# A gather by the one-hot as weights, with h split ahead in the projection, in a two-layer trunk with experts

## Chip, cores and metric

The kernel runs on one core of one Trainium2 chip. The metric is device time in microseconds (us) of one execution; three executions of the kernel before are shown, and one profiled execution.

## The reference, cut to what matters

Two layers, each a mixer (layer 0: gated linear attention beside a state-space head group; layer 1: a gated recurrence beside latent attention) and then a channel mixer with 16 experts, of which each of the 256 tokens takes two. x is 256 x 1024.

```python
for layer in (0, 1):
    h = h + g1 * mixer(modulate(h, norm_mix, sh1, sc1))
    xt = modulate(h, norm_ffn, sh2, sc2)              # rms_norm(h) * gain * (1 + scale) + shift
    scores = sigmoid(xt @ router_w)                   # 16 experts; best group of four, then top 2
    combine = normalized weights of the two experts
    for e in range(16):
        hid = silu(xt @ w_gate[e]) * (xt @ w_up[e])
        out += combine[:, e:e+1] * (hid @ w_down[e])
    h = h + g2 * out
```

## The kernel before

All weights come from HBM through one queue, SP's, into a ring of slots of 1 MB (`Stream`, L227). A slot is asked for when the program frees an older one, up to a cap that each stage sets (L20), and if a stretch of the work area is free. Weights of an expert stage are 96 slots: 16 experts with gate, up and down, two slots each. The first three experts have fixed places; the order of the other 13 follows from the routing, so their loads are issued only when 13 numbers have been read into SP's registers (L2030).

The two mixers are scheduled by the compiler; the parts under `manual()` (L303), and so the whole of `moe` (L1904), keep the order in which the program issues them, engine by engine.

`out_proj` (L790) ends a mixer: products in two precisions parts into four banks (token half t, column half c), then `add` (L808) scales them, adds them to h and squares the new h for the norm. `moe` then turns h (L1922), forms the router's logits, the norm's factors `rs`, the routing (L1776) with ranks within each expert, and splits h times `rs` into a high and a low part of reduced-precision type (L1948, L1951). `late` (L545) takes conditioning products (L540) in between.

The experts are worked off in seven passes of 128 token places (L29): two experts with 64 places each, or four with 32, and so on. Pass p has these steps. `one_hot` (L1989) marks on VectorE which token stands in which place, one pass ahead. `gather` (L2009) brings the tokens of the next pass in as columns: for each of eight blocks of 128 features four products (high and low part, two token halves) with h as weights and the one-hot as the moving operand, then scale and shift by feature (L2022, L2024) into `x3`. `hidden` (L2058) makes the gate and up products (L2066), each expert on its own columns of the array, and the gated activation. Between gate and up stands `spread(1)` of the pass before, which puts its results back to the tokens (L2123) and adds them to h (L2124). `turned` (L2083) transposes the one-hot and the hidden rows (L2095, L2096). `down` (L2098) makes the down products of one column half (L2106), scales them (L2109) and splits them in two parts (L2111, L2112). The loop over passes (L2237) has the order: one_hot of the pass after the next, hidden, turned, gather of features 0 to 511, down 0, gather of features 512 to 1023, spread(0), down 1. In the last pass a branch (L2225) is taken or not by a number read at run time, for tokens beyond an expert's places; it has further passes of the same kind (L2131), which don't occur with these inputs.

Of the kernel before, what the change touches and what calls it, by code (L numbers as in the profile page):

```python
# [18 lines left out]
ARENA, ARENAR, ARENAX = 34048, 6144, 5376  # L19
MIX0_CAP, MIX1_CAP, ODD_CAP, PRE_CAP, MOE_CAP = 7, 6, 11, 12, 18  # L20
# [149 lines left out]
class Arena:  # L170
# [6 lines left out]
    def alloc(self, n):  # L177

        fit = [(o + w - n < self.floor, w, -o, i) for i, (o, w) in enumerate(self.free_) if w >= n]
        if not fit:  # L180
            raise RuntimeError('arena full: %d of %s' % (n, self.free_))
        _, w, o, i = min(fit)
        self.free_[i:i + 1] = [(-o, w - n)] if w > n else []
        return Buf(self, w - o - n, n)
# [113 lines left out]
class Trunk:  # L298
# [56 lines left out]
    def sources(self):  # L355
# [13 lines left out]
        def moe(l):  # L369

            def add(place, e, hf):
                c = slice(2048 * hf, 2048 * hf + 2048)

                def late():
                    if self.eids.get(l) is None:
# [87 lines left out]
    def setup(self):  # L463
# [27 lines left out]
        self.cos, self.sin = T(64, 'cos'), T(64, 'sin')  # L491

# [143 lines left out]

    def rstd(self):
        self.nc.vector.scalar_tensor_tensor(self.ss, self.hsq[0], EPS, self.hsq[1], op0=ALU.add, op1=ALU.add)  # L638
        self.pow(self.rs2, self.ss, self.mhalf)
# [126 lines left out]
    def mixer_input(self, x, tmp):  # L766

        nc = self.nc
        self.xhb, self.xlb = self.newx(2048), self.newx(2048)
# [12 lines left out]

    def input_done(self):

        self.x2 = Rot(self.rx, 256, 3), Rot(self.rx, 256, 2)
        self.xhb.free()
        self.xlb.free()
        self.x2[1].b.append(self.newx(256))

    def out_proj(self, nk, mix, hook):  # L790
# [84 lines left out]
    def even_head(self):  # L875
# [24 lines left out]
        self.xhb, self.xlb = self.newx(2048), self.newx(2048)  # L900
# [26 lines left out]
    def even(self):  # L927
# [371 lines left out]
        def hook(k):  # L1299
# [79 lines left out]
    def odd(self):  # L1379
        nc, W, A, new = self.nc, self.W, self.A, self.new  # L1380
        mm, V, S, G = nc.tensor.matmul, nc.vector, nc.scalar, nc.gpsimd
        ident = self.ident
        lwa, lwx = new(1024), new(1024)
        nc.sync.dma_start(lwa.f, A['lwa'])
        nc.sync.dma_start(lwx.f, A['lwx'])
        stat = new(192)
# [82 lines left out]
        ktok, krt, vb = [new(1024) for _ in range(2)], [new(512) for _ in range(2)], new(2048)  # L1469
# [179 lines left out]
        def attn_c(h):  # L1649
# [5 lines left out]
            mix[8 + h] = new(256)  # L1655
# [7 lines left out]
        def lru_gates(f, x):  # L1663
            lb[f] = ab, qb, ub, gb = [new(256) for _ in range(4)]
# [106 lines left out]
        for b in mix.values():  # L1771
            b.free()
# [3 lines left out]
    def route(self, pl, wk, then):  # L1776
# [17 lines left out]
        then()  # L1794
# [44 lines left out]
        key2, cmp, big, res = tmp(NDYN), tmp(n2), tmp(2 * n2), tmp(NDYN)  # L1839
# [64 lines left out]
    def moe(self, l):  # L1904
        nc, W, new = self.nc, self.W, self.new
        mm, V, S, G = nc.tensor.matmul, nc.vector, nc.scalar, nc.gpsimd
        region = self.region('xm%d' % l, 6400)
# [10 lines left out]
        ht, lgs, wk = newf(2048), newf(256), new(800)  # L1918
# [29 lines left out]
        def high(t):  # L1948
            S.activation(hs[0][:, t], self.h[:, t], AF.Identity, scale=self.rs[t])

        def low(t):  # L1951
            V.scalar_tensor_tensor(hs[1][:, t], self.h[:, t], self.rs[t], hh.v(2)[:, t], op0=ALU.mult, op1=ALU.subtract)

# [13 lines left out]
        total(0)  # L1967
        rstd(1)
# [33 lines left out]
        oh = one_hot(0, s3)  # L2002
        low(0)
        low(1)
        xg = newf(1024)
        yh, yl = newx(512), newx(512)
        mcol = self.mcol2

        def gather(one, js=(0, 1), act=False):  # L2009

            ps = [self.ps('gat') for _ in js]
            for q, (t, h) in enumerate((t, h) for h in hs for t in range(2)):
                for j, p in zip(js, ps):
                    for i in range(4):
                        d = slice(128 * (4 * j + i), 128 * (4 * j + i) + 128)
                        mm(p[:, 128 * i:128 * i + 128], h[:, t, d], one[:, t, :], start=q + i == 0, stop=q + i == 6)  # L2016
            for j, p in zip(js, ps):
                for i in range(4):
                    c = 32 * i + j
                    d, x, sc, sh = x3[:, 4 * j + i], p[:, 128 * i:128 * i + 128], mcol[:, c + 8:c + 9], mcol[:, c + 6:c + 7]  # L2020
                    if j and not act:
                        V.tensor_scalar(d, x, sc, sh, op0=ALU.mult, op1=ALU.add)  # L2022
                    else:
                        S.activation(d, x, AF.Identity, scale=sc, bias=sh)  # L2024
        x3 = xg.v(8)
        gather(oh.v(2, True), act=True)
# [11 lines left out]
        wk.free()  # L2038
        hd, htb, uscb = new(512), new(512), new(160)
# [58 lines left out]
        def down(p, c, parts=1):  # L2098

            ws = [weight(base[p] + j, 'wd', c) for j in range(len(PASSES[p]))]  # L2100
            n = 512 // parts
            for i in range(parts):
                py = self.ps('y')
# [4 lines left out]
                s = slice(n * i, n * i + n)  # L2108
                V.scalar_tensor_tensor(xo.f[:, s], py[:, 0:n], self.wc, self.g[:, 512 * c + n * i:512 * c + n * i + n],  # L2109
                                       op0=ALU.mult, op1=ALU.mult)  # L2110
                S.activation(yh.r[:, s], xo.f[:, s], AF.Copy)  # L2111
                V.tensor_tensor(yl.r[:, s], xo.f[:, s], yh.f[:, s], op=ALU.subtract)  # L2112
            W.free(*ws)

# [16 lines left out]
        def unit_hidden(u, ws, ub):  # L2131
# [5 lines left out]
            m, x, su, cu = usc[:, 0:16], usc[:, 16:48], usc[:, 48:50], usc[:, 50:52]  # L2137
# [9 lines left out]
            for t in range(2):  # L2147
                V.tensor_scalar(one[:, t].rearrange('p (j s) -> p j s', j=2),
                                iota[:, 0:64].unsqueeze(1).to_broadcast([128, 2, 64]), su[:, t:t + 1], None, op0=ALU.is_equal)
            for c in range(2):  # L2150
# [6 lines left out]
                if c:  # L2157
                    V.tensor_copy(xu[64:128], p[64:128])
                else:
                    S.activation(xu[0:64], p[0:64], AF.Copy)  # L2160
# [113 lines left out]
        for r in (hh, hl, hd, htb, uscb):  # L2274
# [20 lines left out]
```

## Time and profile before

| what | value |
|---|---|
| three executions | 900.54 us median (899.21 to 900.74) |
| profiled execution | 900.47 us, its span 898.7 us |
| TensorE (PE) busy | 828.0 us, 92% of the span |
| VectorE (DVE) busy | 481.9 us, 54% |
| ScalarE (ACT) busy | 296.8 us, 33% |
| SP's weight queue (q1) | 303.78 MB, 84.0% of 16 engines' span |
| granted TensorE clock | 0.967 of full speed, mean |

Busy times are unions over the span; PE's ends are modelled, so of two products behind each other the starts are the safer measure. PEld is the load of weights into the array, which lies beside products. In a timeline an arrow in brackets gives the idle time of the engine ahead of the instruction and what ended it. In views by stretch PEclk is the granted share of TensorE's full clock, DMA the mean busy share of 16 DMA engines.

### The profile page before, as it was taken

The numbers are of one execution on the slowest core, as the hardware profiler recorded it, in microseconds if no ns is written. First come the engines' busy times: TensorE is split into PE (matmuls) and PEld (weight loads), VectorE is DVE, ScalarE is ACT, GpSimd is POOL, SyncE is SP. The second block draws the span as 40 slices with busy tenths as digits, with TensorE's granted clock in tenths as the row PEclk, the third lists the DMA queues.
The fourth block names the chain that finished last, engine by engine and source line by source line (L and its number), as shares of the span: only waits on it lengthen the run. The fifth ranks groups of instructions, "written<-read, shape, count | busy, mean of one in ns | idle before, by whom it ended". The sixth has DMA issues, their size and how long they took to land. (4 is left out here: it accounts for less than half of the span.)

```text
span 898.7 us, 13799 instructions
## 1 busy us (share of the span) xinstructions
PE 828.0 (92%) x5202; PEld 515.1 (57%) x5202; DVE 481.9 (54%) x1081; ACT 296.8 (33%) x593; POOL 121.6 (14%) x123
## 2 busy tenths in 40 slices
PE   4797999999899999999779899999989999999976
PEld 1686878768543444354248678998845444345422
DVE  3599856986713531233137688998672342233313
ACT  3354335544320111011034468997332111111100
POOL 0044344431000000000004620112100000000000
PEclk9899999999999999999899899999988999999988
DMA  9992786698889999999989388234979999999994
GB/s 373 417 419 108 286 332 261 226 370 332 320 343 421 421 421 419 421 421 420 417 323 389 101 342 353 94 115 135 357 304 420 422 420 420 421 420 421 422 416 178
DMA packets 44431, 306.02 MB, mean 341 GB/s; under 512 B 5057, under 2 KB 5953, under 8 KB 8513
## 3 DMA queue, kind: packets, MB, share of 16 engines
q1 hardware_dynamic: 43344, 303.78, 84.0%
q10 hardware_dynamic: 1008, 1.24, 0.4%
q8 instruction: 44, 0.72, 0.3%
q14 instruction: 35, 0.28, 0.1%
HBM read 303.95 MB, written 1.05 MB: 339 GB/s over the span
## 5 line engine op out<-in xcount | busy, mean ns | idle before, releaser
L2106 PE MATMUL y<-arena 128*64 128x512 f32 (+3 forms) x592 | 109.1, 577 | 4.1 <-DMA arena<-wd 2.7
L2109 DVE SCALAR_TENSOR_TENSOR arena<-y,wc,g 128x512 f32<-128x512 f32 (+1 forms) x30 | 21.5, 716 | 108.8 <-PE y L2106 108.8
L2106 PEld LDWEIGHTS y<-arena 128*32 128x32 f32 (+2 forms) x592 | 34.0, 132 | 61.7 <-issue 48.0
L692 DVE TENSOR_TENSOR x0r<-arena,x0r 128x1024 fp32r<-128x1024 f32 x40 | 56.1, 1404 | 14.8 <-ACT x0r L691 9.5
L2111 ACT ACTIVATE xm<-arena 128x512 fp32r<-128x512 f32 (+1 forms) x30 | 18.1, 602 | 135.6 <-DVE arena L2109 135.6
L2016 PEld LDWEIGHTS gat<-xm 128*128 128x128 f32 x448 | 55.4, 202 | 12.1 <-issue 12.1
L2074 DVE TENSOR_TENSOR arena<-arena,up 128x512 f32<-128x512 f32 x14 | 9.6, 688 | 96.9 <-PE up L2066 96.9
L692 DVE TENSOR_TENSOR x1r<-arena,x1r 128x1024 fp32r<-128x1024 f32 (+3 forms) x52 | 54.4, 1059 | 9.5 <-POOL x1r L689 4.6
L2016 PE MATMUL gat<-xm 128*128 128x128 f32 x448 | 59.3, 289 | 0.0
L2066 PE MATMUL up<-arena,xm0f 128*64 128x512 f32 (+2 forms) x224 | 52.0, 631 | 5.9 <-DVEq L2225 5.9
L2066 PE MATMUL up<-arena,xm1f 128*64 128x512 f32 (+2 forms) x224 | 51.7, 627 | 5.9 <-DVEq L2225 5.9
L2096 ACT ACTIVATE arena<-hidt 128x512 f32<-128x512 f32 x14 | 8.4, 599 | 139.5 <-PE hidt L2095 139.5
L2066 PE MATMUL gate<-arena,xm1f 128*32 128x512 f32 (+2 forms) x240 | 47.2, 604 | 0.0
L2071 DVE SCALAR_TENSOR_TENSOR arena<-arena,gate 128x512 f32<-128x512 f32 x14 | 9.6, 687 | 69.6 <-ACT arena L2070 58.6
L800 PE MATMUL op<-x1r,x 128*128 128x512 f32 x192 | 46.6, 396 | 0.0
L2066 PE MATMUL gate<-arena,xm0f 128*32 128x512 f32 (+2 forms) x240 | 46.1, 594 | 0.1
L691 ACT ACTIVATE x1r<-arena 128x1024 fp32r<-128x1024 f32 (+3 forms) x42 | 37.3, 902 | 22.7 <-PE kv L764 7.5
L2123 PE MATMUL mo<-xm 128*128 128x512 f32 (+1 forms) x120 | 38.5, 421 | 5.6 <-ACT xm L2111 3.9
L540 PE MATMUL adaps<-arena,cpad 128*32 128x512 f32 x320 | 41.6, 640 | 0.0
L619 POOL TENSOR_TENSOR rs<-ss,mhalf 128x1 f32<-128x1 f32 (+1 forms) x6 | 4.5, 750 | 271.0 <-DVE ss L638 246.7
L800 PEld LDWEIGHTS op<-x1r,x 128*128 128x128 f32 x192 | 35.1, 188 | 8.0 <-issue 0.5
L742 PE MATMUL xbc<-x,x0r 128*128 128x256 f32 x264 | 34.1, 286 | 4.8 <-DVE arena L846 2.9
(461 smaller groups left out, 1588.4 us busy)
## 6 DMA issues: line engine op xcount, KB each, us to landing
arena<-wd SPq DMA_DIRECT2D x62, 1024.0 KB, 15.3
arena<-wg SPq DMA_DIRECT2D x56, 1024.0 KB, 12.9
arena<-wu SPq DMA_DIRECT2D x54, 1024.0 KB, 14.1
arena<-ada SPq DMA_DIRECT2D x48, 1024.0 KB, 8.2
arena<-evin SPq DMA_DIRECT2D x16, 1024.0 KB, 11.1
arena<-odout SPq DMA_DIRECT2D x8, 1024.0 KB, 4.8
arena<-odin SPq DMA_DIRECT2D x8, 1024.0 KB, 11.6
arena<-evout SPq DMA_DIRECT2D x6, 1024.0 KB, 5.9
```

Of the source, the lines that this page charges most:

```text
L540: i = self.nc.tensor.matmul(self.aps[32 * k4:32 * k4 + 32, :], self.cpad[:, 32 * (4 * hf + k4) + 31 - n:32 * (4 * hf + k4) + 63 - n], b.f[ ...
L691: nc.scalar.activation(hi, w, AF.Copy)
L692: (nc.gpsimd if d == 'P' else nc.vector).tensor_tensor(lo, w, hi.bitcast(F32), op=ALU.subtract)
L742: self.nc.tensor.matmul(p[:, c0:c0 + 256], a[:, 128 * k:128 * k + 128], b[:, k, :], start=n == 0, stop=n == 23)
L800: nc.tensor.matmul(acc[t][c], x[a][:, ts], w[b][:, 512 * c:512 * c + 512], start=f and k == 0, stop=l and k == nk - 1)
L2016: mm(p[:, 128 * i:128 * i + 128], h[:, t, d], one[:, t, :], start=q + i == 0, stop=q + i == 6)
L2066: mm(ph[o:o + w, :], x(4 * hf + k)[:, o:o + w], ws[j].f[:, 512 * k:512 * k + 512], start=hf + k == 0, stop=hf == 1 and k == 3)
L2071: V.scalar_tensor_tensor(hd.f, hd.f, 1.0, ph, op0=ALU.add, op1=ALU.mult)
L2106: mm(py[o:o + w, 0:n], ht[:, 128 * f + o:128 * f + o + w], ws[j].f[:, 512 * f + n * i:512 * f + n * i + n], start=f == 0, stop=f == 3)
L2109: V.scalar_tensor_tensor(xo.f[:, s], py[:, 0:n], self.wc, self.g[:, 512 * c + n * i:512 * c + n * i + n], op0=ALU.mult, op1=ALU.mult)
L2111: S.activation(yh.r[:, s], xo.f[:, s], AF.Copy)
L2123: mm(po[:, 0:n], cw[:, 128 * t:128 * t + 128], y.r[:, n * i:n * i + n], start=j == 0, stop=j == 1)
```

## The change

Six edits, in the words of the code. (1) `out_proj`'s `add` splits the new h of three of its four quarters into parts by itself, without `rs`; the fourth is split in `moe`. The parts live in a buffer of 4096 columns that the mixers' inputs also use. (2) `scales` makes the norm's factor by place, with the one-hot as weights (two products of one column and a copy); `pick` gathers with the one-hot as weights (four products of 512 columns) and multiplies by that factor; `place` transposes (four) and applies scale and shift. (3) In the loop, `pick` and `place` stand where `gather` stood, `spread(0)` moves behind the second down product, and the end of that product (`y1`) behind `spread(0)`. (4) The conditioning products of the stage's head come all ahead of the routing. (5) The register load is split in one and twelve, each followed by issues. (6) The second mixer's products get one block, some of its buffers other homes, and the ring's cap in the projections is 14.

```diff
-ARENA, ARENAR, ARENAX = 34048, 6144, 5376
-MIX0_CAP, MIX1_CAP, ODD_CAP, PRE_CAP, MOE_CAP = 7, 6, 11, 12, 18
+ARENA, ARENAR, ARENAX = 34048, 6144, 1280
+MIX0_CAP, MIX1_CAP, ODD_CAP, PRE_CAP, MOE_CAP = 7, 6, 11, 14, 18
...
+        self.rsg = T(2, 'rsg')
+        self.kr = Arena(keep.tile([128, 4096], F32R, name='xhl'), 4096, True)
+        self.hp = [Buf(self.kr, 2048 * i, 2048) for i in range(2)]
...
+    def parts(self, t, c):
+
+        s = slice(512 * c, 512 * c + 512)
+        self.split(*[b.v(2, True)[:, t, s] for b in self.hp], self.h[:, t, s])
...
             if t + c < 2:
                 self.square(t, c, acc[t][c])
+                self.parts(t, c)
...
-                W.set_cap(PRE_CAP + 2)
+                W.set_cap(PRE_CAP)
...
+        mixb = self.ar.alloc(4096, True)
+        mixs = [Buf(self.ar, mixb.o + 256 * i, 256) for i in range(16)]
...
-            mix[8 + h] = new(256)
+            mix[8 + h] = mixs[8 + h]
...
-            lb[f] = ab, qb, ub, gb = [new(256) for _ in range(4)]
+            lb[f] = ab, qb, ub, gb = [self.ar.alloc(256, f > 2) for _ in range(3)] + [mixs[f]]
...
-        hh, hl = self.newr(2048), self.newr(2048)
-        hs = (hh.v(2, True), hl.v(2, True))
+        hs = [b.v(2, True) for b in self.hp]
...
         total(0)
+        S.activation(hs[0][:, 1, 512:1024], self.h[:, 1, 512:1024], AF.Copy)
         rstd(1)
...
-        self.late(2)
-
-        def highs():
-            for t in range(2):
-                high(t)
-        sort, combine = self.route(pl[:, 0:32], wk.f, highs)
         self.late(99)
+        sort, combine = self.route(pl[:, 0:32], wk.f)
...
-        oh = one_hot(0, s3)
-        low(0)
-        low(1)
...
+        def scales(dst, one):
+
+            p = self.ps('rsg')
+            for t in range(2):
+                mm(p[:, 0:1], one[:, t], self.rs[t], start=t == 0, stop=t == 1)
+            V.tensor_copy(dst, p[:, 0:1])
+
+        def pick(p, c, xt, act):
+
+            one, pg, r = oh2[p % 2].v(2, True), self.ps('gat'), rsg[:, p % 2:p % 2 + 1]
+            for q, (t, h) in enumerate((t, h) for t in range(2) for h in hs):
+                mm(pg, one[:, t], h[:, t, 512 * c:512 * c + 512], start=q == 0, stop=q == 3)
+            if act:
+                S.activation(xt, pg, AF.Identity, scale=r)
+            else:
+                V.tensor_scalar(xt, pg, r, None, op0=ALU.mult)
+
+        def place(c, xt, act):
+
+            pt = self.ps('xt')
+            for i in range(4):
+                nc.tensor.transpose(pt[:, 128 * i:128 * i + 128], xt[:, 128 * i:128 * i + 128], self.ident)
+            for i in range(4):
+                o = 32 * i + c
+                d, x, sc, sh = x3[:, 4 * c + i], pt[:, 128 * i:128 * i + 128], mcol[:, o + 8:o + 9], mcol[:, o + 6:o + 7]
+                if act:
+                    S.activation(d, x, AF.Identity, scale=sc, bias=sh)
+                else:
+                    V.tensor_scalar(d, x, sc, sh, op0=ALU.mult, op1=ALU.add)
+        one_hot(0, s3)
+        scales(rsg[:, 0:1], oh2[0].v(2))
+        V.tensor_tensor(hs[1][:, 1, 512:1024], self.h[:, 1, 512:1024], self.hp[0].v(2)[:, 1, 512:1024], op=ALU.subtract)
+        pick(0, 0, self.mod, True)
+        pick(0, 1, t1.f, False)
+        place(0, self.mod, True)
+        place(1, t1.f, True)
         sort()
...
-        self.eids[l] = regs(self.cnt[0:1, 0:NDYN], engines=SP, min_val=0, max_val=15)[1]
-        W.fill()
+        self.eids[l] = []
+        for a, b in ((0, 1), (1, NDYN)):
+            self.eids[l] += regs(self.cnt[0:1, a:b], engines=SP, min_val=0, max_val=15)[1]
+            W.fill()
         one_hot(1)
+        scales(rsg[:, 1:2], oh2[1].v(2))
...
-        def down(p, c, parts=1):
+        def down(p, c, parts=1, later=False):
...
+                if not later:
+                    end()
             W.free(*ws)
+            return end
...
             if 0 < p < last:
                 one_hot(p + 1)
+                scales(rsg[:, (p + 1) % 2:(p + 1) % 2 + 1], oh2[(p + 1) % 2].v(2))
...
             if p < last:
-                gather(oh2[(p + 1) % 2].v(2, True), (0,))
+                pick(p + 1, 0, self.mod, True)
             down(p, 0)
             if p < last:
-                gather(oh2[(p + 1) % 2].v(2, True), (1,))
-            spread(0, cw, p == last)
-            down(p, 1, 2 if p == last else 1)
+                place(0, self.mod, True)
+                pick(p + 1, 1, self.mod, False)
+                y1 = down(p, 1, later=True)
+                place(1, self.mod, False)
+                spread(0, cw)
+                y1()
+            else:
+                spread(0, cw, True)
+                down(p, 1, 2)
             before = cw
```

## Rows read from the trace of the kernel before

**Rows 1.** Busy time by stretch, middle of the first expert stage, columns as in the view's head.
```profile
core 0: us, PE busy (x) PEld busy (x) DVE busy (x) ACT busy (x) POOL busy (x), PEclk, DMA share, GB/s
255.00:345.00 90.00, 88.99 (x518) 38.90 (x518) 30.11 (x76) 12.13 (x25) 0.00 (x0) 1.00 1.01 421
```

**Rows 2.** What TensorE waited for, 246 to 460 and 680 to 900: total us, times, longest.
```profile
PE y L2106 <- DMA arena<-wd: 1.8, 2, 1.4
...
PE y L2106 <- DMA arena<-wd: 0.9, 1, 0.9
```

**Rows 3.** Timeline, change from pass 1 to pass 2 of layer 0: start us, length us, engine, line.
```profile
292.67 0.66 PE L2095 MATMUL hidt<-consts,arena 128*128 128x128 f32 x4
...
293.08 1.98 PE L2016 MATMUL gat<-xm 128*128 128x128 f32 x16
...
293.37 0.60 ACT L2096 ACTIVATE arena<-hidt 128x512 f32<-128x512 f32 x1 [9.01 <-PE hidt L2095]
...
300.78 1.36 DVE L2022 TENSOR_SCALAR xm0f<-gat,mcol 128x128 f32<-128x128 f32 x4
...
301.81 3.65 PE L2106 MATMUL y<-arena 128*64 128x512 f32 x16
302.06 1.28 DVE L2124 TENSOR_TENSOR h<-mo,h 128x512 f32<-128x512 f32 x2
305.29 7.04 PE L2066 MATMUL gate<-arena,xm0f 128*64 128x512 f32 x32
```

**Rows 4.** Timeline, the routing of layer 0 on TensorE and of layer 1 on VectorE.
```profile
238.98 0.20 PE L1829 MATMUL rank<-ob,c 128*128 128x16 bf16 x1 [2.83 <-DVE ob L1826]
...
239.27 3.29 PE L540 MATMUL adaps<-arena,cpad 128*32 128x512 f32 x16
...
682.92 0.69 DVE L659 TENSOR_TENSOR modlo<-modrow,modhi 128x512 fp32r<-128x512 f32 x1 [5.37 <-ACT modhi L658]
683.53 0.18 DVE L1868 SCALAR_TENSOR_TENSOR arena<-arena,ob 128x32 f32<-128x32 f32 x1
```

**Rows 5.** Timeline, pass 1 of layer 0, from the end of pass 0 to its up products.
```profile
276.92 0.75 DVE L2109 SCALAR_TENSOR_TENSOR arena<-y,wc,g 128x512 f32<-128x512 f32 x1 [2.20 <-PE y L2106]
...
279.04 0.49 DVE L1997 TENSOR_TENSOR xm<-pslot,consts 128x128 fp32r<-128x128 f32 x2
...
283.64 1.20 PE L2123 MATMUL mo<-xm 128*128 128x512 f32 x4
...
284.77 7.09 PE L2066 MATMUL up<-arena,xm0f 128*64 128x512 f32 x32
```

**Rows 6.** Busy time by stretch: the last pass, and the end of the routing, of layer 0.
```profile
432.50:450.00 17.50, 10.78 (x87) 3.40 (x86) 2.60 (x6) 0.46 (x1) 0.00 (x0) 0.80 1.01 416
...
247.50:250.00 2.50, 2.50 (x14) 0.86 (x12) 1.12 (x4) 1.26 (x4) 0.00 (x0) 1.00 0.04 10
```

**Rows 7.** Timeline of TensorE, last pass of layer 0.
```profile
438.44 1.07 PE L2066 MATMUL up<-arena,xm0f 128*32 128x512 f32 x3 [5.93 <-DVEq L2225]
...
447.91 0.44 PE L2080 MATMUL cw<-consts,xm 128*128 128x128 f32 x2
...
455.37 0.50 PE L2123 MATMUL mo<-xm 128*128 128x512 f32 x1 [1.54 <-ACT xm L2111]
...
456.99 5.35 PE L2106 MATMUL y<-arena 128*32 128x256 f32 x64
```

**Rows 8.** Timeline, first gather and first gate products, layer 0, then layer 1.
```profile
240.01 2.47 DVE L1952 SCALAR_TENSOR_TENSOR xm<-h,rs,xm 128x1024 fp32r<-128x1024 f32 x2
...
246.10 0.49 DVE L1997 TENSOR_TENSOR xm<-pslot,consts 128x128 fp32r<-128x128 f32 x2
...
246.38 7.09 PE L2066 MATMUL gate<-arena,xm0f 128*64 128x512 f32 x32
...
673.20 7.09 PE L2016 MATMUL gat<-xm 128*128 128x128 f32 x32
...
676.46 0.50 DVE L1997 TENSOR_TENSOR xm<-pslot,consts 128x128 fp32r<-128x128 f32 x2
...
680.22 8.15 PE L2066 MATMUL gate<-arena,xm1f 128*64 128x512 f32 x32
```

More of the change, by code (lines that the diff above doesn't have):

```diff
@@ L175, in __init__, with alloc @@
         self.given = [(0, 0, cols)]
-    def alloc(self, n):
-        fit = [(o + w - n < self.floor, w, -o, i) for i, (o, w) in enumerate(self.free_) if w >= n]
+    def alloc(self, n, last=False):
+        fit = [(o + w - n < self.floor, 0 if last else w, -o, i) for i, (o, w) in enumerate(self.free_) if w >= n]
         if not fit:
@@ L182, in alloc @@
         _, w, o, i = min(fit)
+        w = self.free_[i][1]
         self.free_[i:i + 1] = [(-o, w - n)] if w > n else []
@@ L374, in late @@
                 def late():
-                    if self.eids.get(l) is None:
+                    if len(self.eids.get(l, ())) <= place - STATIC:
                         return None
@@ L768, in mixer_input @@
         nc = self.nc
-        self.xhb, self.xlb = self.newx(2048), self.newx(2048)
+        self.xhb, self.xlb = self.kr.alloc(2048), self.kr.alloc(2048)
         self.xh, self.xl = self.xhb.v(8, True), self.xlb.v(8, True)
@@ L787, in input_done @@
         self.xlb.free()
-        self.x2[1].b.append(self.newx(256))
+        self.x2[1].b.append(self.kr.alloc(256))
     def out_proj(self, nk, mix, hook):
@@ L899, in even_head @@
         nc = self.nc
-        self.xhb, self.xlb = self.newx(2048), self.newx(2048)
+        self.xhb, self.xlb = self.kr.alloc(2048), self.kr.alloc(2048)
         self.xh, self.xl = self.xhb.v(8, True), self.xlb.v(8, True)
@@ L1385, in odd @@
         nc.sync.dma_start(lwx.f, A['lwx'])
-        stat = new(192)
+        stat = self.ar.alloc(192, True)
         st = stat.f
@@ L1468, in odd @@
         self.tail()
-        ktok, krt, vb = [new(1024) for _ in range(2)], [new(512) for _ in range(2)], new(2048)
+        ktok, krt, vb = [new(1024) for _ in range(2)], [new(512) for _ in range(2)], self.ar.alloc(2048, True)
         v3 = vb.v(2)
@@ L1770, in odd, with route @@
         self.out_proj(16, lambda k: mix[order[k]].f, hook)
-        for b in mix.values():
-            b.free()
+        mixb.free()
         self.end_phase()
-    def route(self, pl, wk, then):
+    def route(self, pl, wk):
         nc, V, S = self.nc, self.nc.vector, self.nc.scalar
@@ L1793, in route @@
         S.activation(th, th, AF.Tanh, scale=0.5)
-        then()
         V.scalar_tensor_tensor(d3(sel), d3(th), 0.5, self.bias16.unsqueeze(1).to_broadcast([128, 2, 16]),
@@ L1838, in route @@
         n2 = NDYN * NDYN
-        key2, cmp, big, res = tmp(NDYN), tmp(n2), tmp(2 * n2), tmp(NDYN)
+        cmp, big, key2, res = tmp(n2), tmp(2 * n2), kb[:, 0:NDYN], v[:, 0:NDYN]
         sq = lambda a: a.rearrange('p (a b) -> p a b', a=NDYN)
@@ L1906, in moe @@
         mm, V, S, G = nc.tensor.matmul, nc.vector, nc.scalar, nc.gpsimd
-        region = self.region('xm%d' % l, 6400)
+        region = self.region('xm%d' % l, 2304)
         newx, newf = self.newx, self.fx.alloc
         self.dump('h%d' % (1 + 2 * l), flat(self.h))
-        hh, hl = self.newr(2048), self.newr(2048)
-        hs = (hh.v(2, True), hl.v(2, True))
+        hs = [b.v(2, True) for b in self.hp]
         W.more = self.fx
@@ L1917, in moe @@
         oho = newx(256)
-        ht, lgs, wk = newf(2048), newf(256), new(800)
+        ht, lgs, wk, t1 = newf(2048), newf(256), new(768), new(512)
         pl, lg = self.ps('logit'), self.ps('logits')
@@ L1946, in total @@
             mm(pl[:, 16 * t:16 * t + 16], d, self.cst('lsel'), start=True, stop=True)
[L1948 to L1952, printed above, removed]
         def rstd(t):
@@ L2001, in one_hot @@
             return o
-        oh = one_hot(0, s3)
-        low(0)
-        low(1)
-        xg = newf(1024)
+        xg, rsg = newf(1024), self.rsg
         yh, yl = newx(512), newx(512)
[L2007 to L2024, printed above, removed]
@@ L2025, in moe @@
-        x3 = xg.v(8)
-        gather(oh.v(2, True), act=True)
+        mcol, x3 = self.mcol2, xg.v(8)
+        def scales(dst, one):
[11 more added lines that the diff above has]
+                V.tensor_scalar(xt, pg, r, None, op0=ALU.mult)
@@ L2038, in moe @@
         wk.free()
+        t1.free()
         hd, htb, uscb = new(512), new(512), new(160)
@@ L2096, in turned, with end @@
             S.activation(ht, pt, AF.Copy)
-        def down(p, c, parts=1):
+        def down(p, c, parts=1, later=False):
             ws = [weight(base[p] + j, 'wd', c) for j in range(len(PASSES[p]))]
             n = 512 // parts
+            def end():
+                V.scalar_tensor_tensor(xo.f[:, s], py[:, 0:n], self.wc, self.g[:, 512 * c + n * i:512 * c + n * i + n],
+                                       op0=ALU.mult, op1=ALU.mult)
+                S.activation(yh.r[:, s], xo.f[:, s], AF.Copy)
+                V.tensor_tensor(yl.r[:, s], xo.f[:, s], yh.f[:, s], op=ALU.subtract)
             for i in range(parts):
-                py = self.ps('y')
+                py, s = self.ps('y'), slice(n * i, n * i + n)
                 for f in range(4):
@@ L2107, in down @@
                            ws[j].f[:, 512 * f + n * i:512 * f + n * i + n], start=f == 0, stop=f == 3)
[L2108 to L2112, printed above, removed]
+                if not later:
+                    end()
             W.free(*ws)
+            return end
         def spread(c, cw, last=False, parts=1):
@@ L2136, in unit_hidden @@
             ow = hd2.rearrange('p (t s) -> p t s', t=2)
-            m, x, su, cu = usc[:, 0:16], usc[:, 16:48], usc[:, 48:50], usc[:, 50:52]
+            m, x, su, cu, ru = usc[:, 0:16], usc[:, 16:48], usc[:, 48:50], usc[:, 50:52], usc[:, 52:53]
             x3, m3 = x.rearrange('p (t e) -> p t e', t=2), m.unsqueeze(1).to_broadcast([128, 2, 16])
@@ L2149, in unit_hidden @@
                                 iota[:, 0:64].unsqueeze(1).to_broadcast([128, 2, 64]), su[:, t:t + 1], None, op0=ALU.is_equal)
+            scales(ru, ohu)
             for c in range(2):
@@ L2157, in unit_hidden @@
                 if c:
-                    V.tensor_copy(xu[64:128], p[64:128])
+                    V.tensor_scalar(xu[64:128], p[64:128], ru[64:128], None, op0=ALU.mult)
                 else:
-                    S.activation(xu[0:64], p[0:64], AF.Copy)
+                    S.activation(xu[0:64], p[0:64], AF.Identity, scale=ru[0:64])
             for t in range(2):
@@ L2273, in moe @@
         W.more = None
-        for r in (hh, hl, hd, htb, uscb):
+        for r in (hd, htb, uscb):
             r.free()
```

## The prediction

> **What bounds the kernel now.** I looked first at stretches of the expert stages, then at who waits for whom there, then at the timeline of one change of pass. In the long middle of the first expert stage TensorE is busy for 88.99 of 90 us at full clock while the DMA engines run at 1.01 and 421 GB/s [rows 1]: two resources look full. The waits say which one sets the pace. TensorE waits for a weight transfer for 1.8 us in the whole first stage and 0.9 us in the second [rows 2]. So TensorE's chain is the bound and the transfers keep up only just; one ring slot of 1024 KB takes about 2.5 us at 421 GB/s. Anything that holds TensorE between two passes is paid in full. The timeline shows that nothing holds it now: from the transposes of the hidden rows of one pass (292.67) to the first gate product of the next (305.29) are 12.62 us, without a gap worth naming [rows 3].
>
> **Each engine keeps the written order in these stages.** The second 16 conditioning products (L540) have nothing to do with the rank products ahead of them, yet they start at 239.27, behind rank products that sat 2.83 us waiting for VectorE. On VectorE, L1868 needs the scores alone, yet it starts at 683.53, behind L659, which waited 5.37 us for ScalarE [rows 4]. This decides the forecast, because the change puts two small products, which wait for VectorE, ahead of each pass.
>
> **Part one: gather, place, and the new order of a pass change.** Removed are 32 products of 128 columns per pass. Added are 8 of 512 columns, 8 transposes, one more 128x512 copy on ScalarE and one on VectorE, and the row scales. On TensorE, start to start: four transposes 0.41 (292.67 to 293.08), four products of 512 columns 1.13 (283.64 to 284.77), a down product 3.48 (301.81 to 305.29) [rows 3, 5]. The new row of work is transposes, four picks, down product, four transposes, four picks, down product: 0.41 + 1.13 + 3.48 + 0.41 + 1.13 + 3.48 = 10.04 us. Four transposes and spread(0) then add 0.41 + 1.13, so without a wait the next gate product would come at 11.58, 1.04 earlier than now. All that the copies cost lies beside the down products.
>
> Now the wait. At the start of passes 1 to 5 one_hot(p+1) and scales come ahead of hidden(p). The scale products need the one-hot, and VectorE reaches it only behind the end of the old pass, which the change makes later. Counted from the end of the second down product: 0.70 until the first transposed copy can start (292.67 to 293.37), 1.36 for place(1)'s four copies, 1.28 for the two additions of spread(0) [rows 3], then y1() and the one-hot, which today take 2.61 from the start of L2109 to the end of L1997 (276.92 to 279.53, ScalarE's rounding among it) [rows 5], then 0.05 for the hand-over and 0.2 for two scale products, the time of two of the four transposes, the nearest row for products that have one column and a full set of weights. That is 6.2 us, of which TensorE works 1.54 ahead of the wait. The gate product comes at 10.04 + 6.2 = 16.24 instead of 12.62: **3.6 us later**, and TensorE stands still for about 4.5. What queues behind the waiting product is all of hidden(p), and SP's refill behind its releases. Passes 1 to 5 in two layers make ten such waits: **+36**. The sixth change (into the last pass) has none: 2 x -1.04 = **-2.1**. By bounds: if additions and copies overlap better than written, 2.8 each; with 0.1 more at each of five hand-overs, 4.1.
>
> **Part two: the clock behind each wait.** Today one wait of 5.93 us lies in the last pass. The granted clock of that stretch is 0.80 on average [rows 6], and the up products run from 438.44 to 447.91, 9.47 us where 7.09 is usual [rows 5, 7]: 2.4 us lost, at 1.2 in place of 2.4 GHz. Behind a wait of 1.54 us a down product, in two halves, takes 5.35 us in place of some 3.5 [rows 3, 7]: 1.8 lost. A wait of 4.5 us lies between the two, so I take 1.9 for each of ten: **+19**, with 0 and 24 as ends. The Trainium skill, TensorE: Matmul & The Clock Gate, section "HAM oscillation — how this bites in real kernels", says that a wait that recurs between bursts of products sends the clock down each time anew; it speaks against this change. By that rule all ten falls are paid and the sum is the forecast; if the clock stayed up it would be the first rival's.
>
> **Part three: the head of each stage.** Between one-hot and sort VectorE has 2.47 us of low parts (L1952) today; in their place come the scale copy, one subtraction, and a copy that waits for both picks. In layer 0: 0.3 for scales, 2.26 for eight picks, 0.3 hand-over, 0.69 copy, so the sort starts 1.2 later. The first gate product no longer starts beside one_hot(1) (246.38 against 246.10) but behind it and the next scales: one_hot at 247.3, gate at about 248.1, **+1.7** [rows 8]. In layer 1 the clock is at 1.2 GHz there (gather 7.09, first gate 8.15 us), so the picks cost 4.5 and one_hot goes from 676.46 to about 680.2: gate at 681.2, **+1.0** [rows 8]. A first gate behind a wait of 3.5 us loses clock too: +1.9, and +0.8 where 1.06 is lost already. The parts taken in the output projection add three copies (0.60 as L2096) and three subtractions (0.64 to 0.69) per layer; TensorE's products of the other quarters hide them, and where that cover ends one pair, 1.3, lies ahead of the last transposes. I take 0.5 per layer, **+1.0** in all. Bounds for the head: -3 (its own work is shorter and the products fewer) to +9; sum **+6.4**.
>
> **What I cost at nothing.** The products of the second mixer in one block, the new homes of buffers, 14 slots, the split register load on SP: they can bring weights earlier, but TensorE would then hardly wait for weights anyway. What is gone with the slower passes are today's own waits for weights, 1.8 + 0.9: **-2.7**. If the cover failed, two slots, 5.0 us, would be the price or the gain.
>
> **The sum.** 36 - 2.1 + 19 + 6.4 - 2.7 = +56.6, on the profiled execution's 900.47 us (span 898.7, 1.8 around it; the median of the runs, 900.54, is the same): **957 us**.
>
> **Rivals.**
> *The waits stand, the clock does not fall.* For it: 4.5 us is shorter than 5.93, and the gate products start at once behind the wait. Against: the 1.54 us wait that did cost. 957 - 19 - 2.7 (the head's share) = **935**. Chance 0.25.
> *Transfers are the bound, and the scales wait beside them.* This is the other side: faster. Place: the end of each routing, where DMA stands at 0.04 for 2.5 us [rows 6]. The first placed expert is then asked for after one register instead of thirteen, which fills these 2.4 us in layer 0, and two more slots in layer 1 leave, as an estimate, 2 of their 5.0 once the later sort is paid. 900.5 - 4.4 = **896**. It decides if TensorE would have to wait for weights by more than 3.6 us per pass; the rows show 1.8 and 0.9 in whole stages. Chance 0.08.
> *The scales don't hold TensorE,* because the one-hot is taken ahead of the old pass's end. The order in the text speaks against it, and so do rows 4. Twelve changes of pass would give 12 x 1.04 back, of which the transfers let through about what they gain: **896** too. Chance 0.04.
> *The gather's gain and the wait cancel* (a wait of about 1 us): 900, chance 0.02.
> The forecast keeps 0.61.
>
> **The numbers.** Low: ten waits at 2.8, no clock loss, no head: 28 - 2.1 - 2.7 = +23, 924. High: 41 - 2.1 + 24 + 8 = +71, 971. Slower holds forecast and first rival with some margin, 0.87; same 0.02; faster 0.11. About 0.2% (1.8 us) is what a measurement of this kernel can tell from no change.
>
> **What would show it.** Right: between passes TensorE idle for 4 to 5 us, ended by VectorE's L1997, ten times; the granted clock of the expert stages below 1.00; gate products of 8 to 9.5 us behind each wait; DMA's share below 1 in the middle of the stages; no wait for weights. Wrong: the first gate product of a pass directly behind spread(0), DMA still at 1.01 through both stages, or a first gate ahead of 246.

## The result, and the profile after

The kernel after takes 951.3 us (median of four, 950.46 to 953.15) beside 899.88 for the kernel before (four, 898.65 to 900.74): a ratio of 1.0575, 95% interval 1.0554 to 1.0597. It is slower by 51 us; 957 had been forecast. The profiled execution took 951.33 us, its span 949.2.

The same 90 us of the first expert stage as in [rows 1], then a piece behind one change of pass, by the view of stretches (PE, PEld, DVE, ACT and POOL busy, granted share of TensorE's clock, DMA share, GB/s):

```profile
255.00:345.00 90.00, 80.92 (x380) 32.71 (x378) 26.66 (x69) 13.88 (x28) 0.00 (x0) 0.94 0.91 370
...
320.00:322.90 2.90, 2.90 (x10) 0.75 (x8) 0.00 (x0) 0.00 (x0) 0.00 (x0) 0.51 0.76 314
```

TensorE is busy for 80.92 us where it was 88.99, and neither the clock (0.94, was 1.00) nor the DMA engines (0.91, was 1.01) are full any more, so the rate of neither sets the pace here. In the 2.9 us of the second line TensorE works without a gap at 0.51 of its clock, the lower of its two levels.

What TensorE waited for in the two expert stages, 240 to 500 and 690 to 960 (total us, times, longest), beside [rows 2]:

```profile
PE rsg L2009 <- DVE xm L1996: 24.6, 7, 4.3
...
PE rsg L2009 <- DVE xm L1996: 24.8, 7, 4.3
```

The waits of TensorE for weights are gone from the list. In their place stand, in each layer, seven waits of one line: the scale products L2009 for VectorE's one-hot L1996, five of them at changes of pass and two in the head. The timeline of the change from pass 1 to pass 2 of layer 0, the place of [rows 3]:

```profile
302.96 0.66 PE L2113 MATMUL hidt<-consts,arena 128*128 128x128 f32 x4
...
309.57 3.65 PE L2130 MATMUL y<-arena 128*64 128x512 f32 x16
...
313.57 1.18 PE L2145 MATMUL mo<-xm 128*128 128x512 f32 x4
...
315.14 1.28 DVE L2146 TENSOR_TENSOR h<-mo,h 128x512 f32<-128x512 f32 x2
316.33 0.74 DVE L2122 SCALAR_TENSOR_TENSOR arena<-y,wc,g 128x512 f32<-128x512 f32 x1
317.19 0.63 ACT L2124 ACTIVATE xm<-arena 128x512 fp32r<-128x512 f32 x1 [6.17 <-DVE arena L2122]
317.85 0.69 DVE L2125 TENSOR_TENSOR xm<-arena,xm 128x512 fp32r<-128x512 f32 x1 [0.78 <-ACT xm L2124]
318.46 0.49 DVE L1996 TENSOR_TENSOR xm<-pslot,consts 128x128 fp32r<-128x128 f32 x2
318.89 0.58 PE L2009 MATMUL rsg<-rs,xm 128*128 128x1 f32 x4 [4.14 <-DVE xm L1996]
319.39 8.78 PE L2084 MATMUL gate<-arena,xm0f 128*64 128x512 f32 x32
```

TensorE has done its own work at 314.75 and stands until 318.89, while VectorE walks through the additions, the end of the down product and only then the one-hot. From the transposes of the hidden rows to the next gate product (below: hidden rows to gate) are 16.43 us, where it was 12.62. The gate product then takes 8.78 instead of 7.04, since half of it runs at the lower clock.

### The profile page after: what moved, and what is told of

It reads as the page before. It is cut to its first block, busy times and chain, and to the rows that moved or that the text cites. A ratio compares the mean times of both kernels' runs of the same rounds, so it can differ in the third digit from the quotient of the medians.

```text
span 949.2 us, 13525 instructions
## 1 busy us (share of the span) xinstructions
PE 837.7 (88%) x5034; PEld 506.0 (53%) x5034; DVE 493.1 (52%) x1113; ACT 305.5 (32%) x611; POOL 121.6 (13%) x123
## 5 line engine op out<-in xcount | busy, mean ns | idle before, releaser
L2130 PE MATMUL y<-arena 128*64 128x512 f32 (+3 forms) x592 | 105.3, 576 | 1.4 <-ACT arena L2114 1.4
L2084 PE MATMUL gate<-arena,xm0f 128*32 128x512 f32 (+2 forms) x240 | 57.1, 692 | 0.2 <-issue 0.2
L2084 PE MATMUL gate<-arena,xm1f 128*32 128x512 f32 (+2 forms) x240 | 55.0, 676 | 0.0
L2009 PE MATMUL rsg<-rs,xm 128*128 128x1 f32 x56 | 10.1, 285 | 49.3 <-DVE xm L1996 49.3
L2088 ACT ACTIVATE arena<-gate 128x512 f32<-128x512 f32 x14 | 8.4, 599 | 131.8 <-PE gate L2084 131.8
L809 PE MATMUL op<-x1r,x 128*128 128x512 f32 x172 | 43.5, 397 | 0.0
L751 PE MATMUL xbc<-xhl,x0r 128*128 128x256 f32 x264 | 36.5, 299 | 3.7 <-DVE arena L856 3.0
L2145 PE MATMUL mo<-xm 128*128 128x512 f32 (+1 forms) x120 | 35.5, 412 | 4.5 <-ACT xm L2124 3.9
L2009 PEld LDWEIGHTS rsg<-rs,xm 128*128 128x128 f32 x56 | 9.2, 233 | 54.2 <-issue 38.1
```

The costliest lines, as they stand in the source:

```text
L751: self.nc.tensor.matmul(p[:, c0:c0 + 256], a[:, 128 * k:128 * k + 128], b[:, k, :], start=n == 0, stop=n == 23)
L809: nc.tensor.matmul(acc[t][c], x[a][:, ts], w[b][:, 512 * c:512 * c + 512], start=f and k == 0, stop=l and k == nk - 1)
L2009: mm(p[:, 0:1], one[:, t], self.rs[t], start=t == 0, stop=t == 1)
L2084: mm(ph[o:o + w, :], x(4 * hf + k)[:, o:o + w], ws[j].f[:, 512 * k:512 * k + 512], start=hf + k == 0, stop=hf == 1 and k == 3)
L2130: mm(py[o:o + w, 0:n], ht[:, 128 * f + o:128 * f + o + w], ws[j].f[:, 512 * f + n * i:512 * f + n * i + n], start=f == 0, stop=f == 3)
L2145: mm(po[:, 0:n], cw[:, 128 * t:128 * t + 128], y.r[:, n * i:n * i + n], start=j == 0, stop=j == 1)
```

## The experiments

Eleven kernels, each timed beside the kernel before. In four of them (e1, e2, f3, f4) only the place of a few instructions in the kernel after is changed; e4 and g2 put one part of the change into the kernel before. **Theory A** is the prediction's: the scale products hold TensorE's queue behind VectorE, and the clock falls behind each hold. **Rival B**: the new gather costs the time. **Rival C**: the transfers do. The counts of falls below are each from one profiled execution.

**e1, the scale products moved to where the one-hot is long there.**

```diff
         one_hot(1)
-        scales(rsg[:, 1:2], oh2[1].v(2))
...
             if 0 < p < last:
                 one_hot(p + 1)
-                scales(rsg[:, (p + 1) % 2:(p + 1) % 2 + 1], oh2[(p + 1) % 2].v(2))
...
             if p < last:
+                scales(rsg[:, (p + 1) % 2:(p + 1) % 2 + 1], oh2[(p + 1) % 2].v(2))
                 pick(p + 1, 0, self.mod, True)
```

> Edit: in the kernel after, the scale products and their copy move from the start of a pass to just ahead of the first pick, where the one-hot is long there; the head's scales for pass 1 move with them. Theory A (the scale products hold TensorE's queue behind VectorE's one-hot, and the clock falls behind each wait): hidden rows to next gate product 11.8 + 0.5 = 12.3 us instead of 16.4, ten times, -41; clock -17; first gates -4 in each layer: 885 us, 882 to 897 if the transfers then hold it a little; granted clock 1.00 in the middle of the expert stages. Rival B (the new gather itself, with its transposes and copies, costs the time): above 940. Rival C (transfers come later and hold TensorE): above 930, with waits for weights.

Measured: 895.95 us (894.53 to 898.05), ratio to before 0.9958 (0.9944 to 0.9973). The same stretch as above, then the change of pass, then TensorE at the end of pass 3:

```profile
255.00:345.00 90.00, 88.89 (x502) 35.41 (x499) 32.43 (x82) 13.60 (x27) 0.00 (x0) 1.00 1.01 418
```

```profile
289.09 0.66 PE L2112 MATMUL hidt<-consts,arena 128*128 128x128 f32 x4
289.58 0.50 PE L2009 MATMUL rsg<-rs,xm 128*128 128x1 f32 x4
...
301.26 7.09 PE L2083 MATMUL gate<-arena,xm0f 128*64 128x512 f32 x32
...
352.44 3.62 PE L2129 MATMUL y<-arena 128*32 128x512 f32 x26 [1.51 <-DMA arena<-wd]
...
359.87 1.05 PE L2129 MATMUL y<-arena 128*32 128x512 f32 x2 [1.30 <-DMA arena<-wd]
362.37 3.62 PE L2129 MATMUL y<-arena 128*32 128x512 f32 x26 [1.45 <-DMA arena<-wd]
```

Moving these few instructions gives back 55 us, and the kernel is then faster than the one before. B falls: the new gather, with its transposes and copies, is all still there. From hidden rows to gate are now 12.17 us, and the gate runs at full clock. But the time lies at the upper end of A's range, and the last three lines say why: in pass 3, which takes four experts' weights in the time of two, TensorE waits for down weights. The next gate comes 20.5 us behind the hidden rows in both layers, where 12.2 is usual: 8.4 held by transfers, twice. So C is wrong for the kernel after; of the repaired one it names what now holds it.

**e4, the other way round: the kernel before, with the scale products alone** (their result unused; `scales` itself is as in the kernel after).

```diff
             if 0 < p < last:
                 one_hot(p + 1)
+                scales(rsg[:, (p + 1) % 2:(p + 1) % 2 + 1], oh2[(p + 1) % 2].v(2))
```

> Edit: the kernel before with one part alone: the two scale products and their copy (unused) behind one_hot at the start of passes 1 to 5; the old gather stays. Theory A: the one-hot ends 3.3 us after the last down product, so TensorE waits 2.9 and works 0.5, ten times, +34; with the clock's fall 1.7 each: 951 us, 934 if the clock stays up. Rival B (the new gather is what costs): the scales' own 0.5 x 10, at most 907.

Measured: 931.16 us, ratio 1.0339 (1.0318 to 1.036). B's bound of 907 is passed by far: two products of one column in the wrong place cost the old kernel 31 us. A's 951 was too much. Two of its ten changes of pass:

```profile
380.91 0.58 PE L2031 MATMUL rsg<-rs,xm 128*128 128x1 f32 x4 [2.69 <-DVE xm L1997]
381.35 8.81 PE L2074 MATMUL gate<-arena,xm0f 128*128 128x512 f32 x16
...
414.04 0.58 PE L2031 MATMUL rsg<-rs,xm 128*128 128x1 f32 x4 [2.79 <-DVE xm L1997]
414.55 3.65 PE L2074 MATMUL gate<-arena,xm0f 128*64 128x512 f32 x16
418.03 3.60 PE L2074 MATMUL gate<-xm0f 128*64 128x512 f32 x16
```

The waits are 2.5 to 2.8 us, and the clock fell behind seven of ten (the first gate above took 8.81, the second 3.65 and 3.60, as usual). From the starts of the gates: ten delays of 3.3 (+33), the clock +12, the old transfer holds ahead of pass 4 gone (-6.5, below), and 7 us less between the last gate of layer 0 and the end of the first of layer 1, where the clock was higher than in the profile of before: +31.

**e2, the wait halved.** The one-hot is taken between spread(0) and y1().

```diff
             if 0 < p < last:
-                one_hot(p + 1)
...
                 spread(0, cw)
+                if p + 1 < last:
+                    one_hot(p + 2)
                 y1()
```

> Edit: in the kernel after, the one-hot is taken on VectorE between spread(0) and the end of the second down product; the scale products stay at the start of the pass. Theory A: the wait of 4.14 us shrinks by the 1.9 us of that end to 2.2, ten times, -19. If the clock still falls behind 2.2 us: 932 us, and gate products of 8.6 to 8.8. If it stays up: 915, gate products of 7.1. Rival B (the new gather costs the time): 949 to 953.

Measured: 918.6 us, ratio 1.0232 (1.0173 to 1.029), between A's two values. Two changes of pass:

```profile
311.83 0.58 PE L2009 MATMUL rsg<-rs,xm 128*128 128x1 f32 x4 [2.02 <-DVE xm L1996]
312.33 7.09 PE L2084 MATMUL gate<-arena,xm0f 128*64 128x512 f32 x32
...
402.66 0.61 PE L2009 MATMUL rsg<-rs,xm 128*128 128x1 f32 x4 [2.13 <-DVE xm L1996]
403.20 5.35 PE L2084 MATMUL gate<-arena,xm0f 128*64 128x512 f32 x16
```

Behind ten waits of 2.0 to 2.1 us the clock fell three times. One of the four executions took 927.16 us at a mean clock of 0.950, where the other three (916.25 to 918.72) have 0.964, so what the clock takes differs from one execution to the next.

**e3 and g3, the wait filled with work nobody needs,** which leaves the gates as late as they were and takes only the standing still away.

```diff
...
             p = self.ps('rsg')
+            for i in range(12 if fill else 0):
+                mm(p, fill[:, i % 2], hs[i % 2][:, i % 2, 0:512], start=True, stop=True)
             for t in range(2):
```

> Edit: in the kernel after, twelve products of 512 columns, whose results nobody reads, stand ahead of the scale products of each pass change, 3.5 of the 4.14 us of the wait. Theory A with the clock as a term of its own: the gates start as late as before, hidden rows to gate 16.4, but the clock stays at 1.00 and gate products take 7.1: 951.3 - 10 x 1.7 = 934 us. Rival D (gate products behind a wait are longer for another cause, or the clock does not decide): 950 or more.

> Edit: as e3 with seventeen products ahead of the scale products instead of twelve, so that of the wait of 4.14 us some 0.1 is left instead of 1.32. Theory A (it is the standing still that lets the clock fall): the three falls of e3 in ten go too, the gates come when they did: 936.2 - 3 x 1.7 = 931 us, all ten gate products at 7.0. Rival (the falls of e3 come from something else, the one-column products or the chain's own rhythm): 936, with two to four falls left.

Measured: 936.22 us with twelve products (1.0402, 1.0385 to 1.042), 930.81 with seventeen (1.0341, 1.0316 to 1.0366). The same change of pass in e3, then in g3:

```profile
310.18 2.90 PE L2009 MATMUL rsg<-xhl,xm 128*128 128x512 f32 x12
314.40 0.61 PE L2011 MATMUL rsg<-rs,xm 128*128 128x1 f32 x4 [1.32 <-DVE xm L1996]
314.94 8.78 PE L2086 MATMUL gate<-arena,xm0f 128*64 128x512 f32 x32
```

```profile
313.51 4.04 PE L2009 MATMUL rsg<-xhl,xm 128*128 128x512 f32 x17
317.74 0.61 PE L2011 MATMUL rsg<-rs,xm 128*128 128x1 f32 x4 [0.19 <-DVE xm L1996]
318.27 7.09 PE L2086 MATMUL gate<-arena,xm0f 128*64 128x512 f32 x32
```

With 1.3 to 1.5 us of standing still left, three falls in ten; with 0.2 to 0.4, none. The gates come 16.4 behind the hidden rows in both, as in the kernel after. So the clock is a term of its own: with work that nobody needs in its waits, the kernel is 20.5 us faster here. By the lengths of the gate products 17 of them lie behind the ten waits. 3.1 more lie between the two expert stages (251.57 us from last gate to first, 254.70 in the kernel after), where both run the same instructions; these are not shown to come from the edit.

**f4, VectorE's order alone.** The scale products stay at the start of the pass; the one-hot goes ahead of `place(1)`, and the head's scale products move as in f3.

```diff
             if 0 < p < last:
-                one_hot(p + 1)
...
+                if p + 1 < last:
+                    one_hot(p + 2)
                 place(1, self.mod, False)
                 spread(0, cw)
```

> Edit: the kernel after with VectorE's order alone changed at the pass changes: the one-hot is taken ahead of the second placing, so that it is long there when the scale products come at the start of the pass, where they stay; the head's as in f3. Theory A (what counts is that the one-hot stood behind the old pass's end on VectorE, not where TensorE makes the scale products): as e1, 896 us, 894 to 898, no wait ahead of the scale products, no fall of the clock. Rival (the scale products at the start of a pass cost by themselves, by a change of weights or a switch of type): above 905.

Measured: 898.52 us (894.7 to 900.35), ratio 0.9986 (0.9972 to 1.0001); half a microsecond above A's range. The same change of pass:

```profile
301.15 0.50 PE L2009 MATMUL rsg<-rs,xm 128*128 128x1 f32 x4
301.58 7.09 PE L2083 MATMUL gate<-arena,xm0f 128*64 128x512 f32 x32
```

No wait stands ahead of the scale products and no clock falls behind them; hidden rows to gate are 12.06. Either of the two orders can be mended, TensorE's or VectorE's. That this one is 2.6 us behind e1 by medians is left open; the spans of the two profiled runs are the same, 896.3.

**f3, the head's share.** Only the scale products for pass 1 leave the head; those of the passes stay.

> Edit: the kernel after with the head's scale products for pass 1 alone moved behind the first pass's hidden rows; those of passes 1 to 5 stay at the start of their pass. Theory A: the first gate of each layer no longer waits for the second one-hot: 3.7 us in layer 0 and 3.9 in layer 1 by the difference between e2 and e1, and 1.4 of clock each: 951.3 - 10.4 = 941 us. Rival (the first gate is then held by its own tokens or by weights instead): 948 to 952.

Measured: 944.27 us, ratio 1.0494 (1.047 to 1.0517): 7 us back instead of 10.4. In layer 0 the first gate comes at 243.77 instead of 248.63 and takes 7.0 instead of 8.6, as expected; the gates of passes 1 and 2, still behind their waits, take 10.0 and 9.1 where the kernel after has 9.3 and 8.7, and from hidden rows to the gate of pass 1 are 20.37 us instead of 18.38. So part of the gain is lost again there, at a granted clock of 0.90 (0.94 in the kernel after).

**f1, f2, g1 and g2, the transfers.** f1 and f2 change the register load of e1 (its twelve later numbers read only behind the first gate products; all thirteen at once). g1 is f1 with the two down slots of the third fixed expert asked for ahead of the first routed expert's. g2 puts the split load alone into the kernel before.

> Edit: the kernel of e1 with the load of the twelve later expert numbers into SP's registers moved behind the first pass's gate products, so that the issues which need only the first number are not queued behind it. Theory T (in e1 the transfers have become the bound: TensorE is held about 8.4 us ahead of pass 4 in each layer, with the DMA engines full all the way): the DMA gap of some 1.8 us ahead of the second issue closes in both layers, and all of it reaches the end: 895.95 - 3.6 = 892 us. Rival U (the hold in pass 3 has another cause, the transfers are not the bound): 895 to 897.

> Edit: the kernel of e1 with edit 5 undone: thirteen numbers loaded at once, then the issues. Theory T: the first two weight slots are asked for 2.2 us or more later and the queue goes on without a gap from there; the DMA engines stand idle some 1 to 2 us longer per layer and all of it reaches the end: 897 to 900 us. Rival U (transfers are not the bound): 895 to 897.

> Edit: the kernel of f1 with the two down slots of the third fixed expert, which need no routing, asked for ahead of the first routed expert's slots, so that the DMA engines have 5 us more to do while the routing runs. Theory T (with the scale products out of the way the transfers are the bound): the engines' idle time around the sort, about 3 us in 245 to 255 of e1, goes in both layers, and the hold ahead of pass 4 (8.4 us in e1) shrinks by as much: 890 us, 888 to 893. Rival U (the hold has another cause): 894 to 896, the hold as long as in e1.

> Edit: the kernel before with edit 5 alone, the register load in one and twelve. The prediction took this edit for nothing. Theory T (the kernel before is already held by transfers ahead of pass 4, 17.26 and 14.69 us from hidden rows to gate where 12.73 is usual): the first two slots come 2 us earlier, the hold shrinks by 1 to 2 us in each layer: 896 to 898 against 899.4. Rival (as predicted, nothing): 899 to 900, within 0.1% of the kernel before.

| kernel | us | ratio to before, 95% |
|---|---|---|
| e1 | 895.95 | 0.9958 (0.9944 to 0.9973) |
| f1 | 894.29 | 0.995 (0.9932 to 0.9969) |
| f2 | 902.31 | 1.0035 (1.0021 to 1.0049) |
| g1 | 891.74 | 0.9908 (0.9885 to 0.9931) |
| g2 | 896.08 | 0.9946 (0.9926 to 0.9966) |

f2 and g1 move by more than the intervals, in the direction of theory T (f2 beyond its 897 to 900), f1 does not. SP's issues in f1 show where its gain stopped:

```profile
246.23 0.95 SPq L249 DMA_DIRECT2D arena<-wg  x2
247.41 1.00 SPq L249 DMA_DIRECT2D arena<-wu  x2
...
258.48 0.34 SPq L249 DMA_DIRECT2D arena<-wg  x1
```

The second pair goes out at 247.41 instead of 253.03, but the slots behind it must first come free, and the next gate weights are asked for at 258.48, in e1 at 258.51. In g1 the down weights of layer 0 arrive 2.2 us earlier (360.17 below, 362.37 in e1), and the lower clock takes it back:

```profile
350.20 3.62 PE L2134 MATMUL y<-arena 128*32 128x512 f32 x26 [1.46 <-DMA arena<-wd]
...
357.69 1.04 PE L2134 MATMUL y<-arena 128*32 128x512 f32 x2 [1.36 <-DMA arena<-wd]
360.17 6.55 PE L2134 MATMUL y<-arena 128*32 128x512 f32 x26 [1.44 <-DMA arena<-wd]
```

The last line has in 6.55 us the 26 products that took 3.62 in e1; the granted clock of its first half was 0.50. The hold of layer 0 thus did not shrink (22.6 us, hidden rows to gate, 20.5 in e1); that of layer 1 fell from 20.5 to 17.3. g1, at 0.9908, beats both kernels. Of g2 the gain is measured, its place is not: the profiled execution, 901.76 us, lies above all its others (893.03 to 898.31), and in it the hold ahead of pass 4 is shorter in layer 0 (13.88 us, was 17.26) and longer in layer 1 (19.03, was 14.69).

## Why the prediction was right, point by point

Working the prediction's terms out from the starts of the gate products, before against after. The rows that carry the transfer hold and the ends, of before and of after:

```profile
350.10 0.66 PE L2095 MATMUL hidt<-consts,arena 128*128 128x128 f32 x4 [0.26 <-DVE arena L2074]
...
352.42 1.06 PE L2106 MATMUL y<-arena 128*32 128x512 f32 x6
353.87 3.62 PE L2106 MATMUL y<-arena 128*32 128x512 f32 x26 [0.39 <-DMA arena<-wd]
357.42 2.00 PE L2016 MATMUL gat<-xm 128*128 128x128 f32 x16
...
360.63 1.74 PE L2106 MATMUL y<-arena 128*32 128x512 f32 x6
363.80 3.62 PE L2106 MATMUL y<-arena 128*32 128x512 f32 x26 [1.44 <-DMA arena<-wd]
367.36 1.13 PE L2066 MATMUL gate<-arena,xm0f 128*128 128x512 f32 x2
...
424.30 4.07 PE L2066 MATMUL gate<-arena,xm0f 128*32 128x512 f32 x36
...
785.75 3.64 PE L2106 MATMUL y<-arena 128*32 128x512 f32 x32
...
855.05 7.07 PE L2066 MATMUL gate<-arena,xm1f 128*32 128x512 f32 x64
```

```profile
247.67 0.95 SPq L249 DMA_DIRECT2D arena<-wg  x2
247.99 0.71 PE L2009 MATMUL rsg<-rs,xm 128*128 128x1 f32 x4 [2.85 <-DVE xm L1996]
248.63 8.62 PE L2084 MATMUL gate<-arena,xm0f 128*64 128x512 f32 x32
...
451.57 7.07 PE L2084 MATMUL gate<-arena,xm0f 128*32 128x512 f32 x64
...
706.27 8.49 PE L2084 MATMUL gate<-arena,xm1f 128*64 128x512 f32 x32
...
905.33 7.07 PE L2084 MATMUL gate<-arena,xm1f 128*32 128x512 f32 x64
```

| term | predicted | measured |
|---|---|---|
| ten waits at changes of pass | +36 | +38.8 |
| sixth change, without a wait | -2.1 | -2.0 |
| clock behind the ten waits | +19 | +17.0 |
| heads, and all else outside the passes | +6.4 | +3.1 |
| own holds by transfers, gone | -2.7 | -6.5 |
| sum | +56.6 | +50.4 |

The spans differ by 50.5. The rows at 424.30 and 855.05, at 451.57 and 905.33 are the gates of the last pass of each layer; from them to the next first gate [rows 8], and to the end, the time outside the passes is counted. The term of the heads is the first gate of layer 0, 2.25 later, the stretch between the stages, 1.2 shorter, the end, 0.2 longer, and the two first gate products, together 1.9 longer.

The sum came out 6 us too high because the terms of the head and of the transfers' holds missed by 3.3 and 3.8 and the clock by 2.0, and the waits, 2.8 the other way, made up for part of it.

*The wait* was right in place, cause and size, ten times. Its 3.88 instead of 3.6 comes mostly from the scale products, which were taken for 0.2 us after the four transposes and take 0.50 from start to start (318.89 to 319.39): four matmuls, not two. VectorE's way, from the end of the second down product (309.57 + 3.48) to the scale products, was 5.84 at the change shown, forecast 6.0. e1, e2 and f4 show the cause by moving it.

*The clock* fell behind all ten, and each fall cost 1.4 to 2.4 us by the length of the gate products, 1.7 on average, against 1.9. The first rival (935, clock stays up) is refuted by the trace, and g3, where it stays up at the changes of pass, though not in the head, measured 930.8. The argument against that rival was weaker than it looked: it rested on one wait of 1.54 us that cost clock [rows 7], and in e3 waits of 1.3 to 1.5 did so three times in ten. The Trainium skill, TensorE: Matmul & The Clock Gate, section "HAM oscillation — how this bites in real kernels", says that a wait that recurs between bursts of products costs clock anew each time. The trace of the kernel after agrees, ten of ten.

*The order.* That a waiting product holds all behind it was argued from [rows 4]; e1 against the kernel after shows it, since with VectorE's one-hot left where it was the gate products come without the wait. The Trainium skill, TensorE: Matmul & The Clock Gate, section "Step-by-step: what each phase is for", says that matmuls stay in program order. The trace agrees: at the change shown the last copies of place(1) end at 315.2, and the gate products stayed behind two products of one column until 319.39.

*The head* was over-sized. The first gate of layer 0 came at 248.63 (forecast 248.1), but from the last gate of layer 0 to the first of layer 1 the new kernel needs 1.2 us less, not more (254.70 against 255.92): in the 22 us around that first gate the granted clock was 0.84, in the profile of before 0.69. That stretch scatters: with the instructions of before it took 255.92 in before and 249.81 in e4, with those of after 254.70 and, in g3, 251.57. With the same head as after, the first gate of layer 0 came at 247.05, 246.90 and 248.96 in e2, e3 and g3, with that of before at 246.38 and, in e4, 246.67. f3 shows that the hold in the head is there: without it the first gate comes at 243.77. How much of this term is the change and how much the clock of those stretches can't be told from one profile of each, and stays open.

*The transfers' holds* were under-sized, and of all terms this one was furthest off. The prediction read them from the view of waits, 1.8 and 0.9 us [rows 2]. The rows of before above show more: two down products, 3.48 each when fed, take 5.00 (352.42 to 357.42) and 6.73 (360.63 to 367.36), and hidden rows to gate are 17.26 where 12.73 is usual, 14.69 in layer 1. That is 6.5 us in all. The view counts the time that TensorE stood, 1.8 in layer 0. The six products that it made ahead of the last weights, 1.06 and 1.74 us, count as work but saved nothing: the 26 behind them take 3.62, as long as a whole down product of 32 when fed (785.75: 3.64).

*What was costed at nothing* was not measured in this kernel: no run takes edit 6, or the split register load, out of the kernel after. There the first routed weights are asked for at 247.67, at 249.86 in the kernel before, and TensorE no longer waits for weights, so little can be left to gain; that is argued, not shown. The split load alone makes the kernel before 3.6 us faster by the medians (g2, 0.3 to 0.7% by the interval), and without it e1 is 6.4 us slower (f2), where 5.0 us had been named as the bound. The second rival (transfers as the bound, 896) thus had its mechanism right for e1: the change's shorter passes (12.17 against 12.62) end in a hold of 8.4 us per layer.

## What to carry to other kernels

A product that is small itself, but stands at the head of a stage, starts only when the latest of its operands is there, and so does all that is queued behind it. Before it is moved or added, look up when the other engine reaches what it waits for. Then price the clock behind the wait by itself; if the wait can't be removed, work that nobody needs can hold the clock up, as in g3. Read a hold from start to start along the chain, since the view of waits shows only the part in which the engine stood still.

## What had not been expected

How often the clock fell goes with the standing still ahead of the gate product, over ten changes of pass in one execution each: ten of 4.14 to 4.26 us (the kernel after, and f3), seven of 2.5 to 2.8 (e4), three of 2.0 to 2.1 (e2), three of 1.3 to 1.5 (e3), none of 0.2 to 0.4 (g3). Equal waits in one run went both ways. Waits for weights did too: in pass 3 of layer 0 three waits of 1.3 to 1.5 us left the clock at 1.00 in e1, while in g1, behind three of 1.4 to 1.5 at the same place, it fell to 0.50, so that weights that came 2.2 us earlier gained nothing there.
